# Three products of the recurrence's preparation issued on VectorE instead of GpSimd, and seven PSUM tiles instead of three for the block products of the first rotary pass

## The chip, the cores and the metric

The kernel runs on one core of a Trainium2 chip. The metric is the device time of one execution in microseconds (us); the time before is the median of three runs. The engines are named as the profile names them: PE is TensorE (PEld its weight loads), DVE is VectorE, ACT is ScalarE, POOL is GpSimd, SP issues the DMAs.

## The reference, cut to what matters

One layer over 2048 latent and 256 context tokens of width 1024: normalisation and modulation, an input projection to 3232 columns, of which 1696 go through a depthwise convolution into a bidirectional RWKV-7 mixer and 1536 into differential attention with rotary queries and keys; an output projection and a gated MLP follow. Two parts are touched.

```python
def apply_rope(x, cos, sin):
    half = DIFF_HEAD // 2
    x1, x2 = x[..., :half], x[..., half:]
    return jnp.concatenate([x1 * cos - x2 * sin, x1 * sin + x2 * cos], axis=-1).astype(x.dtype)
...
# rwkv_prepare, for each of the two directions
w = -jax.nn.softplus(-(w0 + w_lat @ w2).astype(jnp.float32)) - 0.5
decay = jnp.exp(-jnp.exp(w))
a = jax.nn.sigmoid((a0 + al @ a2).astype(jnp.float32))
k_dir = k * (1.0 + (a - 1.0) * p['k_a'])
```

The kernel runs the recurrence in chunks of 64 tokens. So per direction it needs the running products W of the decays within a chunk, their reciprocals IW, and these scaled operands: kk times a and k times (1+(a-1)k_a), both times IW (the tile G), and kk and r times W (the tile Q).

## The kernel before, in words

`phase1` (line 198) makes the normalised, transposed activations in two groups: blocks 0 to 2 (the 256 context tokens and two blocks of 512 latent tokens), later blocks 3 and 4. It projects 128 columns at a time: `wnext` hands out a weight tile split into two parts, `wH` (ACT, L232) and `wL` (POOL, L233), and `mtile` (L244) multiplies it with one block in 24 matmuls (L34 to L36) into a PSUM tile `mm`. The pool of `mm` tiles, `psmm`, has three.

For group 0 come first the columns of the attention's values, then eight column tiles through `rope_tile` (L383), 20 block products. ACT copies four swapped quarters out of `mm` into `rsw` (L401), DVE multiplies `mm` by the cosine (L405), `rsw` by the sine (L406) and adds (L407). `mm` is free after L401 and L405. In the same stretch `mod_chunk` (L124) makes eight pieces of the modulation: DVE accumulates 64 weight tiles `mww` into `macc` (L136), and a small product `mg` (L142, L149) on PE sums each piece over the partitions.

Then come the convolution columns: `tile_a` for blocks 0 to 2, `tile_b` for blocks 3 and 4 and the held-back block 2. ACT evacuates `mm` (L602). `piece` (L544) convolves: ACT one tap (L550), DVE two (L551, L552), into `cout`, or into `okt` for the four column tiles of keys. For a key piece ACT then makes `kk` (L564) and its square `ksq` (L566), PE sums the squares into `pn` (L570), DVE and POOL make the reciprocal norm `krn` (L572, L573), PE spreads it (L578), DVE multiplies (L579). `prep` (L495) follows, once for each direction:

- PE: two small products `pk` (L517); ACT: tanh (L519), sigmoid's shift (L521);
- DVE: the running sum `cs` (L523); ACT: W and IW (L524, L525), the last column of W (L527);
- DVE: first half of `G` (L529); ACT: (1+(a-1)k_a) into `ta` (L530); **POOL: second half of `G` (L531)**; DVE: `G` times IW (L532); SP: `G` to HBM (L533);
- **POOL: `Q` from `kk` (L535)**; ACT: one column of `Q` (L536); **POOL: `Q` from `rr` or `kk` (L537)**; SP: `Q` to HBM (L538).

There are 4 key column tiles and 5 blocks, so 40 directions: 32 with 512 tokens and 8 with the 256 of the context. `G`, `Q` and the inputs `t` have two buffers each.

The second rotary pass (blocks 3 and 4) runs through the same `rope_tile` at the end of `phase1`, while `phase2b` begins. The order in each engine's queue isn't written out: the framework's scheduler sets it when the program is built (L1898), engine by engine, from its own estimate of durations. Each engine then works its queue strictly in order.

Of the kernel before, what the change touches and what calls it, by code (L numbers as in the profile page):

```python
# [8 lines left out]
F32 = mybir.dt.float32  # L9
# [3 lines left out]
ALU = mybir.AluOpType  # L13
AX = mybir.AxisListType
PSUM = bass.MemoryType.PSUM
DRAM = bass.MemoryType.DRAM

P = 128
# [9 lines left out]
BLK = 512  # L28
CH = 64
# [3 lines left out]
def split_mm(nc, out, lH, lL, rH, rL, first, last):  # L33
    nc.tensor.matmul(out, lhsT=lH, rhs=rH, start=first, stop=False)  # L34
    nc.tensor.matmul(out, lhsT=lH, rhs=rL, start=False, stop=False)  # L35
    nc.tensor.matmul(out, lhsT=lL, rhs=rH, start=False, stop=last)  # L36
# [161 lines left out]
def phase1(tc, I, T, pr, ident, bones, keep):  # L198
    nc = tc.nc
    with ExitStack() as st:  # L200
        def rpool(stack, name, bufs, **k):
            return stack.enter_context(tc.tile_pool(name=name, bufs=bufs, side="right", **k))
# [3 lines left out]
        ps = rpool(st, "psmm", 3, space=PSUM)  # L206
# [11 lines left out]
        seq_b = [1536] + [c for j in range(4) for c in (j * P, (4 + j) * P, vcol + j * P, (8 + j) * P)] + [1600] + rope_cols  # L218
        order = v_cols + rope_cols + seq_a + seq_b
        raws, ready = [], []  # L220

        def wload():
            raw = mp.tile([P, KT, P], F32, name="wraw", bufs=1)
            c0 = order.pop(0)
            nc.sync.dma_start(out=raw, in_=wv[:, :, c0:c0 + P])
            raws.append(raw)
# [9 lines left out]
        def wnext():  # L236
            W = ready.pop(0)
            if raws:
                wsplit()
            if order:  # L240
                wload()
            return W

        def mtile(W, b):  # L244
            n = BLOCKS[b][1]
            o = ps.tile([P, BLK], F32, name="mm")
            mtile.out = o
            for k in range(KT):
                split_mm(nc, o[:, 0:n], W[0][:, k], W[1][:, k], hH[b][:, k], hL[b][:, k], k == 0, k == KT - 1)
                if k % 2 and k < KT - 1:  # L250
                    yield

        def mfull(W, b):
            for _ in mtile(W, b):
                pass
            return mtile.out

        def vblock(vp, pv, tags, W, j, b):
            t0, n = BLOCKS[b]
            yield from mtile(W, b)  # L260
            o = mtile.out
            S = vp(tags[0])
            nc.vector.tensor_copy(out=S[:, 0:n], in_=o[:, 0:n])
            yield
            tp = pv.tile([P, BLK], F32, name=tags[1])
            for t in range(n // P):
                nc.tensor.transpose(out=tp[:, t * P:(t + 1) * P], in_=S[:, t * P:(t + 1) * P], identity=ident)
            V = vp(tags[2])
            nc.vector.tensor_copy(out=V[:, 0:n], in_=tp[:, 0:n])
            nc.sync.dma_start(out=T["vd"][t0:t0 + n, j * P:(j + 1) * P].rearrange("(t p) c -> p t c", p=P),  # L270
                              in_=V[:, 0:n].rearrange("p (t c) -> p t c", c=P))
            yield
# [33 lines left out]
        with ExitStack() as s2:  # L306
# [68 lines left out]
            for j in (2, 3):  # L375
                W = wnext()
# [34 lines left out]
        def load_cs(pool, group):  # L411
            lat = [b for b in group if b]
            cs = pool.tile([P, 2, len(lat), BLK], F32, name="cossin")
            nc.sync.dma_start(out=cs, in_=I["rope"][:, :, BLOCKS[lat[0]][0] - CTX:BLOCKS[lat[-1]][0] + BLK - CTX].rearrange("a p (b t) -> p a b t", t=BLK))
            return cs

        with ExitStack() as s4:
            rp = rpool(s4, "ropep", 3)
            rc = rpool(s4, "ropec", 1)
            pv = rpool(s4, "psr", 1, space=PSUM)  # L420
            cs = load_cs(rc, GROUPS[0])
            ones = rc.tile([P, P], F32, name="mones")
            nc.gpsimd.memset(ones, 1.0)

            def mods():
                for part in (2, 3, 4, 5):
                    for hf in range(2):
                        yield from mod_chunk(nc, I, T, col, rp, rc, pv, "mg", sC[:, :, 0], keep, part, hf, ones)
            mg = mods()

            def mstep():
                for _ in range(6):
                    next(mg, None)

            for c0 in rope_cols:
                for _ in rope_tile(c0, GROUPS[0], cs, lambda n: rp.tile([P, BLK], F32, name=n), ("rst", "rsw"), mstep):
                    pass
            nc.sync.dma_start(**late.pop())
            for _ in range(1000):
                next(mg, None)  # L440

        with ExitStack() as s3:
            cp = rpool(s3, "convp", 2)
# [25 lines left out]
            for d, s in enumerate(("fwd", "bwd")):  # L469
# [7 lines left out]
                W = W4[:, d]  # L477
# [17 lines left out]
            def prep(h, b, O, K):  # L495
                t0, n = BLOCKS[b]
                m = n // CH
                rr = K
                if b:
                    rr = cp.tile([P, BLK], F32, name="rr", bufs=2)  # L500
                    nc.sync.dma_start(out=rr, in_=T["rwT"][h * P:(h + 1) * P, t0:t0 + n])
                for d in range(2):
                    i0 = t0 // CH
                    if d:
                        i0 = 0 if b == 0 else 36 + 4 - i0 - m

                    def v(ap):
                        ap = ap[:, 0:n]
                        return ap[:, ::-1] if d else ap

                    def c(ap):
                        return ap[:, 0:n].rearrange("p (m t) -> p m t", t=CH)

                    t = []
                    for e in range(2):
                        z = pv.tile([P, BLK], F32, name="pk")
                        nc.tensor.matmul(z[:, 0:n], lhsT=W4[:, d, e, h * P:(h + 1) * P], rhs=los[b][:, e], start=True, stop=True)  # L517
                        t.append(cp.tile([P, BLK], F32, name="t%d" % e, bufs=2))
                        nc.scalar.activation(out=t[e][:, 0:n], in_=v(z), func=AF.Tanh, scale=0.5)  # L519
                    sg, ta = t  # L520
                    nc.scalar.activation(out=sg[:, 0:n], in_=sg[:, 0:n], func=AF.Identity, scale=0.5, bias=half)  # L521
                    cs = cp.tile([P, BLK], F32, name="cs", bufs=2)
                    nc.vector.tensor_tensor_scan(out=cs[:, 0:n], data0=smask[:, 0:n], data1=sg[:, 0:n], initial=0.0, op0=ALU.mult, op1=ALU.add)  # L523
                    nc.scalar.activation(out=sg[:, 0:n], in_=cs[:, 0:n], func=AF.Exp, scale=-CDEC)  # L524
                    nc.scalar.activation(out=cs[:, 0:n], in_=cs[:, 0:n], func=AF.Exp, scale=CDEC)  # L525
                    W, IW = c(sg), c(cs)
                    nc.scalar.copy(out=pr.wc[:, i0:i0 + m, d, h], in_=W[:, :, CH - 1])  # L527
                    G = cp.tile([P, 2 * BLK], F32, name="G", bufs=2)[:, 0:2 * n].rearrange("p (m e t) -> p m e t", e=2, t=CH)
                    nc.vector.scalar_tensor_tensor(out=G[:, :, 0], in0=c(ta), scalar=1.0, in1=c(v(K)), op0=ALU.add, op1=ALU.mult)  # L529
                    nc.scalar.activation(out=ta[:, 0:n], in_=ta[:, 0:n], func=AF.Identity, scale=hka[:, h:h + 1], bias=oka[:, h:h + 1])  # L530
                    nc.gpsimd.tensor_tensor(out=G[:, :, 1], in0=c(v(O)), in1=c(ta), op=ALU.mult)  # L531
                    nc.vector.tensor_tensor(out=G, in0=G, in1=IW.unsqueeze(2).broadcast_to([P, m, 2, CH]), op=ALU.mult)  # L532
                    nc.sync.dma_start(out=T["pd"][d * 4 + h, :, i0 * P:(i0 + m) * P], in_=G.rearrange("p m e t -> p (m e t)"))  # L533
                    Q = cp.tile([P, 2 * BLK], F32, name="Q", bufs=2)[:, 0:2 * n].rearrange("p (m t) -> p m t", t=P)
                    nc.gpsimd.tensor_tensor(out=Q[:, :, 1:CH], in0=c(v(K))[:, :, 1:CH], in1=W[:, :, 0:CH - 1], op=ALU.mult)  # L535
                    nc.scalar.copy(out=Q[:, :, 0:1], in_=c(v(K))[:, :, 0:1])  # L536
                    nc.gpsimd.tensor_tensor(out=Q[:, :, CH:P], in0=c(v(rr)), in1=W, op=ALU.mult)  # L537
                    nc.sync.dma_start(out=T["qd"][d * 4 + h, :, i0 * P:(i0 + m) * P], in_=Q.rearrange("p m t -> p (m t)"))  # L538
                    yield

# [151 lines left out]
            for c0 in seq_b[1:]:  # L692
                if c0 >= vcol:
                    W = wnext()
# [18 lines left out]
G = 3  # L713
# [243 lines left out]
CH = 64  # L957
# [859 lines left out]
def build(tc, I, out):  # L1817
    nc = tc.nc
    with ExitStack() as st:
# [20 lines left out]
        for ev in phase1(tc, I, T, pr, ident, bones, keep):  # L1840
            if ev == "early":
                next(p2b)
                early = iter(lambda: next(p2b), "main")
            elif early:
                for _ in range(2):
                    next(early, None)
# [55 lines left out]
```

## Time and profile before

| | |
|---|---|
| median of three runs | 4119.32 us (4115.85 to 4120.19) |
| the profiled execution's own time | 4121.25 us |
| its span, first to last instruction | 4119.5 us |
| PE busy | 3798.8 us, 92% |
| DVE, ACT, POOL busy | 63%, 47%, 37% |
| mean granted TensorE clock | 0.955 |

The stages that the change touches, in us from the span's start: first rotary pass 133 to 264; `tile_a` 264 to 470; the transposes of group 1 470 to 540; `tile_b` 540 to 822; second rotary pass 822 to 930. The rows further down give start, busy time of each engine and idle time; in a row of the timeline or of the groups, "idle before" is the time for which the engine stood still just before, and behind "<-" stands what ended it.

### The profile page before, as it was taken

To read this page: it belongs to the slowest core of one execution; us is meant where nothing else is said; L and a number is where in the kernel's file an instruction comes from. 1 tells how busy PE (TensorE), PEld (TensorE's weight loads), DVE (VectorE), ACT (ScalarE), POOL (GpSimd) and SP (SyncE) were. 2 spreads that over 40 slices of the span, in tenths; PEclk is the share of its full clock that TensorE was granted. 3 is DMA by queue.
4 is the path that set the end of the run, shared out by engine and by line. 5 is a ranking of instruction groups with operands and counts; after the bars stand their busy time and mean duration, and the time that the engine had idled before them with its cause. 6 is when DMAs were issued, how large, how long until landed. Compare 5 with 4: busy or idle time off the path is not lost. (4 is left out here: it accounts for less than half of the span.)

```text
span 4119.5 us, 65492 instructions
## 1 busy us (share of the span) xinstructions
PE 3798.8 (92%) x25471; PEld 3218.9 (78%) x25471; DVE 2601.3 (63%) x3781; ACT 1925.6 (47%) x3806; POOL 1511.7 (37%) x1578
## 2 busy tenths in 40 slices
PE   7999888887999886899999889999999999999999
PEld 4777677676888776889898867778888888878887
DVE  3466566778889985888889877754444444420243
ACT  4236556666666655677777744622112112221211
POOL 3236466734444433454544356510111111022222
PEclk8999899998999988999999989999999999999999
DMA  5554546644433433020102164411111111131333
GB/s 175 156 172 163 164 157 220 212 136 96 99 93 97 97 80 97 14 61 9 48 6 63 47 202 137 151 57 45 53 46 54 51 47 47 51 105 50 111 120 104
DMA packets 464724, 400.80 MB, mean 97 GB/s; under 512 B 131613, under 2 KB 393702, under 8 KB 463390
## 3 DMA queue, kind: packets, MB, share of 16 engines
q1 hardware_dynamic: 464414, 396.61, 31.5%
q8 instruction: 201, 3.29, 0.4%
q14 instruction: 109, 0.89, 0.1%
HBM read 269.51 MB, written 131.74 MB: 97 GB/s over the span
## 5 line engine op out<-in xcount | busy, mean ns | idle before, releaser
L34 PE MATMUL o<-h2H,wuH 128*128 128x512 f32 x1920 | 750.9, 392 | 5.7 <-DVE h2H L179 4.0
L35 PE MATMUL o<-h2L,wuH 128*128 128x512 f32 x1920 | 751.4, 391 | 0.4 <-DVE h2L L180 0.2
L36 PE MATMUL o<-h2H,wuL 128*128 128x512 f32 x1920 | 750.4, 391 | 1.2 <-POOL wuL L1607 1.2
L1607 POOL TENSOR_TENSOR wuL<-wuraw,wuH 128x1024 fp32r<-128x1024 f32 x76 | 183.6, 2417 | 840.4 <-ACT wuH L1606 840.4
L34 PEld LDWEIGHTS o<-h2H,wuH 128*128 128x128 f32 x1920 | 361.0, 188 | 84.0 <-DVE h2H L179 4.2
L36 PEld LDWEIGHTS o<-h2H,wuL 128*128 128x128 f32 x1920 | 361.2, 188 | 78.7 <-POOL wuL L1607 1.7
L35 PEld LDWEIGHTS o<-h2L,wuH 128*128 128x128 f32 x1920 | 361.3, 188 | 78.4 <-DVE h2L L180 1.0
L34 PE MATMUL mm<-hH,wH 128*128 128x512 f32 (+1 forms) x968 | 381.4, 395 | 15.6 <-DVE rst L405 9.8
L802 DVE TENSOR_REDUCE nb<-S 128x1 f32<-128x768 f32 x384 | 357.9, 948 | 58.5 <-PE S L801 57.3
L803 ACT ACTIVATE P<-S,nb 128x768 f32<-128x768 f32 x384 | 345.8, 907 | 77.0 <-DVE nb L802 73.9
L35 PE MATMUL mm<-hL,wH 128*128 128x512 f32 (+1 forms) x968 | 378.1, 391 | 0.1
L36 PE MATMUL mm<-hH,wL 128*128 128x512 f32 (+1 forms) x968 | 376.3, 389 | 0.5 <-POOL wL L233 0.5
L800 PE MATMUL S<-kH,qs 128*128 128x384 f32 x768 | 293.5, 382 | 34.9 <-ACT P L803 34.4
L844 PE MATMUL pv<-V,aT 128*128 128x128 f32 x2304 | 309.4, 278 | 6.4 <-DVE O L860 3.3
L1627 ACT COPY cs<-o 128x512 f32<-128x512 f32 x176 | 102.9, 585 | 450.6 <-PE o L36 448.1
L844 PEld LDWEIGHTS pv<-V,aT 128*128 128x128 f32 x2304 | 285.8, 194 | 10.2 <-DVE O L860 6.3
L801 PE MATMUL S<-kL,qs 128*128 128x384 f32 x768 | 261.3, 340 | 0.0
L830 DVE SCALAR_TENSOR_TENSOR P<-P,f,P 128x768 f32<-128x768 f32 x192 | 244.1, 1284 | 12.9 <-POOL P L828 11.6
L34 PEld LDWEIGHTS mm<-hH,wH 128*128 128x128 f32 x968 | 190.7, 198 | 53.4 <-DVE rst L405 10.6
L36 PEld LDWEIGHTS mm<-hH,wL 128*128 128x128 f32 x968 | 190.2, 196 | 37.5 <-issue 1.0
L35 PEld LDWEIGHTS mm<-hL,wH 128*128 128x128 f32 x968 | 191.0, 197 | 35.2 <-issue 0.7
L852 ACT COPY aT<-tpa 128x512 f32<-128x512 f32 (+1 forms) x320 | 173.6, 542 | 93.7 <-PE tpa L851 90.9
(372 smaller groups left out, 8039.2 us busy)
## 6 DMA issues: line engine op xcount, KB each, us to landing
wraw<-in_w_in_dram SPq DMA_DIRECT2D x52, 512.0 KB
wuraw<-in_w_up_dram SPq DMA_DIRECT2D x44, 512.0 KB
scr_actT<-wuH SPq DMA_DIRECT2D x44, 512.0 KB
QP<-scr_qd SPq DMA_DIRECT2D x36, 512.0 KB
PK<-scr_pd SPq DMA_DIRECT2D x144, 128.0 KB
mww<-in_w_mod_dram SPq DMA_DIRECT2D x64, 256.0 KB
scr_qd<-Q SPq DMA_DIRECT2D x32, 512.0 KB
scr_pd<-G SPq DMA_DIRECT2D x32, 512.0 KB
```

The costliest lines, as they stand in the source:

```text
L34: nc.tensor.matmul(out, lhsT=lH, rhs=rH, start=first, stop=False)
L35: nc.tensor.matmul(out, lhsT=lH, rhs=rL, start=False, stop=False)
L36: nc.tensor.matmul(out, lhsT=lL, rhs=rH, start=False, stop=last)
L800: nc.tensor.matmul(S[:, b, 0:HB], lhsT=qs[:, qt * P:(qt + 1) * P], rhs=kH[:, sl], start=True, stop=False)
L801: nc.tensor.matmul(S[:, b, 0:HB], lhsT=qs[:, qt * P:(qt + 1) * P], rhs=kL[:, sl], start=False, stop=True)
L802: nc.vector.tensor_reduce(out=nb[:, m, g:g + 1], in_=S[:, :, 0:HB], op=ALU.max, axis=AX.XY, negate=True)
L803: nc.scalar.activation(out=Pm[m][:, g * GW:(g + 1) * GW].rearrange("p (b x) -> p b x", b=2), in_=S[:, :, 0:HB], func=AF.Exp, bias=nb[:, m, ...
L830: nc.vector.scalar_tensor_tensor(out=Pm[0][:, sls[g - 1]], in0=Pm[0][:, sls[g - 1]], scalar=f[:, 0, g - 1:g], in1=Pm[1][:, sls[g - 1]], op ...
L844: nc.tensor.matmul(pv, lhsT=aT[:, j], rhs=V[:, k0 + j], start=(k0 + j == 0), stop=(k0 + j == KTT - 1))
L852: nc.scalar.copy(out=aT[:, 0:n], in_=tp[:, 0:n])
L1607: eng.tensor_tensor(out=L, in0=raw, in1=H.bitcast(F32), op=ALU.subtract)
L1627: nc.scalar.copy(out=S[:, 1 + b * BLK:1 + (b + 1) * BLK], in_=o)
```

## The change

Three `tensor_tensor` products of `prep` (L531, L535, L537) are issued on DVE instead of POOL, 120 instructions in all. For the first rotary pass alone, `mtile` takes its PSUM tiles in turn from two pools, the three of `psmm` and four of a new pool `psx`; afterwards the list is set back to three.

```diff
         raws, ready = [], []
+        ring = [ps] * 3
...
             n = BLOCKS[b][1]
-            o = ps.tile([P, BLK], F32, name="mm")
+            ring.append(ring.pop(0))
+            o = ring[-1].tile([P, BLK], F32, name="mm")
...
             pv = rpool(s4, "psr", 1, space=PSUM)
+            ring.extend([rpool(s4, "psx", 4, space=PSUM)] * 4)
...
             for _ in range(1000):
                 next(mg, None)
+            ring[:] = [ps] * 3
...
-                    nc.gpsimd.tensor_tensor(out=G[:, :, 1], in0=c(v(O)), in1=c(ta), op=ALU.mult)
+                    nc.vector.tensor_tensor(out=G[:, :, 1], in0=c(v(O)), in1=c(ta), op=ALU.mult)
...
-                    nc.gpsimd.tensor_tensor(out=Q[:, :, 1:CH], in0=c(v(K))[:, :, 1:CH], in1=W[:, :, 0:CH - 1], op=ALU.mult)
+                    nc.vector.tensor_tensor(out=Q[:, :, 1:CH], in0=c(v(K))[:, :, 1:CH], in1=W[:, :, 0:CH - 1], op=ALU.mult)
...
-                    nc.gpsimd.tensor_tensor(out=Q[:, :, CH:P], in0=c(v(rr)), in1=W, op=ALU.mult)
+                    nc.vector.tensor_tensor(out=Q[:, :, CH:P], in0=c(v(rr)), in1=W, op=ALU.mult)
```

The scheduler is run anew, so the queues of all engines are ordered anew. Lines of the changed kernel lie 1 to 4 higher (L531 is L535, L552 is L556). Two places show what moved.

PE, the first rotary pass, the start of the block product that begins at 249.9 us in the trace: `hH_294` is the context block, `hH_360` block 1; a matmul's own wait stands behind it. Before:

```order
L35 MATMUL mm<-hL_295,wH 128x256
L36 MATMUL mm<-hH_294,wL 128x256
L34 MATMUL mm<-hH_360,wH 128x512 [waits DVE_49]
L35 MATMUL mm<-hL_361,wH 128x512
L36 MATMUL mm<-hH_360,wL 128x512
```

The same place of the changed kernel:

```order
L35 MATMUL mm<-hL_295,wH 128x256
L36 MATMUL mm<-hH_294,wL 128x256
L34 MATMUL mm<-hH_360,wH 128x512
L35 MATMUL mm<-hL_361,wH 128x512
L36 MATMUL mm<-hH_360,wL 128x512
```

The order is the same; the wait for DVE is gone. Of the other block products of this pass that waited for DVE alone, one still does (the first into a tile of the new pool); the waits for ACT and POOL at a new weight tile stay.

DVE, `tile_b`, the last rows up to the `okt` row (second tap) of the fourth key tile, for which the next `pn` waits. Before:

```order
L613 COPY kk<-pk 128x512
L523 SCALAR_TENSOR_TENSOR cs<-smask,t_5842 128x512
L529 SCALAR_TENSOR_TENSOR G<-t_5846,kk 128x8x64
L551 SCALAR_TENSOR_TENSOR cout<-cst,cols,cout 128x512
L532 TENSOR_TENSOR G<-G,cs 128x1024
L552 SCALAR_TENSOR_TENSOR cout<-cst,cols,cout 128x512
L551 SCALAR_TENSOR_TENSOR cout<-cst,cols,cout 128x512
L552 SCALAR_TENSOR_TENSOR cout<-cst,cols,cout 128x512
L551 SCALAR_TENSOR_TENSOR cout<-cst,cols,cout 128x512
L552 SCALAR_TENSOR_TENSOR okt<-cst,cols,okt 128x512
```

The same place of the changed kernel:

```order
L555 SCALAR_TENSOR_TENSOR cout<-cst,cols,cout 128x512
L533 SCALAR_TENSOR_TENSOR G<-t_5306,kk 128x8x64
L535 TENSOR_TENSOR G<-okt,t_5281 128x8x64
L556 SCALAR_TENSOR_TENSOR cout<-cst,cols,cout 128x512
L555 SCALAR_TENSOR_TENSOR cout<-cst,cols,cout 128x512
L536 TENSOR_TENSOR G<-G,cs 128x1024
L539 TENSOR_TENSOR Q<-kk,t_5302 128x8x63
L541 TENSOR_TENSOR Q<-rr,t_5302 128x8x64
L555 SCALAR_TENSOR_TENSOR cout<-cst,cols,cout 128x512
L556 SCALAR_TENSOR_TENSOR cout<-cst,cols,cout 128x512
L535 TENSOR_TENSOR G<-okt,t_5306 128x8x64
L556 SCALAR_TENSOR_TENSOR okt<-cst,cols,okt 128x512
```

Four of the moved products stand among the last twelve rows ahead of that `okt` row. From the third `krn` row of the second key tile to the `okt` row of the third, 17 of the tile's 18 moved products stand in DVE's queue. On PE the first `pn` of the second, third and fourth key tile of `tile_b` stands behind 2008, 2200 and 2392 of the 2904 block matmuls before, and behind 2012, 2213 and 2410 now.

## Rows read from the trace of the kernel before

**Rows 1.** The core's span and mean granted clock.

```profile
core 0: 4119.5 us, clock 0.955
```

**Rows 2.** Busy time in stretches; columns: stretch, length, engines (instructions), clock, DMA.

```profile
125.00:300.00 175.00, 158.32 (x730) 130.75 (x729) 103.46 (x132) 59.38 (x94) 41.76 (x28) 0.93 0.57 171
...
349.80:382.00 32.20, 31.32 (x146) 26.29 (x145) 21.65 (x22) 20.74 (x48) 21.97 (x19) 0.89 0.51 174
...
688.60:757.00 68.40, 58.03 (x263) 46.85 (x264) 50.24 (x44) 42.74 (x81) 47.52 (x28) 0.92 0.63 214
```

**Rows 3.** What PE waited for, 125 to 300 us: total, times, longest.

```profile
PE mm L34 <- DVE rst L405: 7.1, 2, 5.5
PE mg L149 <- issue: 5.3, 2, 2.8
PE mg L142 <- issue: 2.9, 1, 2.9
```

**Rows 4.** Timeline of PE in `tile_b`: start, duration, instruction, idle before.

```profile
618.89 1.87 PE L570 MATMUL pn<-bones,ksq 128*128 128x2 f32 x8 [6.09 <-ACT ksq L566]
```

**Rows 5.** Stretches around the two kinds of stop (columns as in Rows 2).

```profile
244.40:249.90 5.50, 0.04 (x1) 0.00 (x0) 3.36 (x3) 3.73 (x6) 2.34 (x1) 0.78 0.53 181
249.90:252.10 2.20, 2.19 (x5) 1.82 (x6) 2.20 (x4) 0.00 (x0) 0.00 (x0) 0.50 0.41 119
252.10:259.00 6.90, 6.90 (x31) 5.71 (x31) 3.83 (x7) 1.21 (x3) 0.47 (x1) 0.84 0.72 193
...
618.80:620.80 2.00, 1.91 (x9) 1.91 (x10) 1.08 (x2) 0.04 (x1) 0.00 (x0) 0.50 1.01 300
620.80:631.00 10.20, 10.20 (x40) 8.29 (x41) 4.14 (x5) 4.95 (x7) 5.71 (x4) 0.73 0.99 349
```

**Rows 6.** Groups of DVE, 125 to 270 us: count, busy, mean ns, idle before.

```profile
L136 DVE SCALAR_TENSOR_TENSOR macc<-mww,sC,macc 128x512 f32<-128x512 f32 x60 | 55.7, 931 | 32.4 <-DMA mww<-in_w_mod_dram 31.5 <-issue 0.3 <-DMA macc<-in_b_mod_dram 0.3
```

**Rows 7.** Timelines of DVE and POOL, some rows where both are busy.

```profile
608.98 1.76 DVE L551 SCALAR_TENSOR_TENSOR cout<-cst,cols,cout 128x512 f32<-128x512 f32 x1
610.66 2.31 DVE L532 TENSOR_TENSOR G<-G,cs 128x1024 f32<-128x1024 f32 x1
...
608.47 1.72 POOL L535 TENSOR_TENSOR Q<-kk,t 128x504 f32<-128x504 f32 x1
610.15 1.73 POOL L537 TENSOR_TENSOR Q<-rr,t 128x512 f32<-128x512 f32 x1
```

**Rows 8.** The same timelines, rows where only one of the two works.

```profile
661.39 1.21 DVE L523 TENSOR_TENSOR_SCAN cs<-smask,t 128x512 f32<-128x512 f32 x1
662.52 0.66 DVE L529 SCALAR_TENSOR_TENSOR G<-t,kk 128x512 f32<-128x512 f32 x1
683.05 0.74 DVE L551 SCALAR_TENSOR_TENSOR cout<-cst,cols,cout 128x512 f32<-128x512 f32 x1
686.48 1.22 DVE L532 TENSOR_TENSOR G<-G,cs 128x1024 f32<-128x1024 f32 x1
...
663.40 1.26 POOL L535 TENSOR_TENSOR Q<-kk,t 128x504 f32<-128x504 f32 x1 [1.72 <-ACT t L524]
```

**Rows 9.** Line 407, a two-input product on DVE: shortest, median, longest ns.

```profile
L407 DVE TENSOR_TENSOR rst<-rst,rsw x32: 651/684/1669, 152.1 to 932.4; 128x512 f32<-128x512 f32 x32
```

**Rows 10.** From the third `krn` to the next `okt`: stretch (columns as in Rows 2).

```profile
637.72:685.90 48.18, 39.02 (x178) 30.45 (x176) 38.44 (x33) 30.20 (x61) 40.61 (x23) 0.98 0.53 183
```

**Rows 11.** The same stretch: a group of POOL, and what DVE waited for.

```profile
L233 POOL TENSOR_TENSOR wL<-wraw,wH 128x1024 fp32r<-128x1024 f32 x3 | 9.4, 3141 | 6.4 <-ACT wH L232 6.3
...
DVE G L529 <- DMA scr_pd<-G: 5.2, 3, 2.6
```

**Rows 12.** Timeline of POOL, a weight split beside little DVE work.

```profile
622.32 2.38 POOL L233 TENSOR_TENSOR wL<-wraw,wH 128x1024 fp32r<-128x1024 f32 x1 [4.02 <-ACT wH L232]
```

## Prediction

> **What bounds the kernel now.** I took the span and the clock first [rows 1], then busy time by stage [rows 2], then PE's waits where the change acts. PE is the busiest engine everywhere, so a microsecond counts only if PE stands still for it or runs slowly after it.
>
> In the first rotary pass PE waits 7.1 us in two places for DVE's cosine product, which frees an `mm` tile, and 8.2 us for the modulation's `mg` products [rows 3]. The longer of the two, 5.5 us, ends at 249.9; the granted clock is 0.50 (1.2 GHz) just after it and 0.84 over the next 6.9 us [rows 5]. That costs 2.2 x 0.50 + 6.9 x 0.16 = 2.2 us more.
>
> In `tile_b` each key column tile takes some 68.4 us, with PE busy 58.0 of them at clock 0.92 [rows 2]. The largest loss is one stop of 6.1 us at `pn` for ACT's `ksq` [rows 4], which came late because DVE's `okt` row did; two of the other three key tiles show the same stop. Behind it the clock is 0.50 for 2.0 us and 0.73 for 10.2 us [rows 5], another 1.0 + 2.75 = 3.75 us. So such a stop costs 9.9 us.
>
> Why is `okt` late? From the third `krn` to the next `okt` row 48.2 us pass, in which DVE is busy 38.4 and POOL 40.6 [rows 10]. Both run long. Where they meet, their instructions take turns: a tap takes 1.76 us and a product on POOL 1.72 to 1.73 [rows 7], against 0.74 and 1.26 where the other engine is quiet [rows 8]. So POOL's products are not free cover. They lengthen DVE's queue.
>
> **The seven tiles.** The order shows that the block product at 249.9 loses its wait for DVE. Its weights were in use already, so nothing else holds it: 5.5 + 2.2 = 7.7 us. The shorter wait, 7.1 - 5.5 = 1.6 us, lies ahead of `mg` products that PE waits for anyway [rows 3], so I count nothing for it. The last `mg` products come earlier on PE too, but their accumulations are paced by loads: DVE stands idle 32.4 us before them in this stretch, 31.5 of it for `mww` [rows 6]. I give 1.7 us back to them and take **6 us**. Bounds: 7.1 + 2.2 = 9.3 us, and nothing if the modulation takes all.
>
> **The three products, tile_b.** Removed from POOL per key tile: 18 products of at least 1.26 us, 22.7 us. Added to DVE: 18 of 0.68, the median of a two-input product of the same size [rows 9], 12.2 us. The moved ones read reversed or strided operands in part; L529 does so already at 0.66 [rows 8].
>
> What matters is the stretch up to `okt`. DVE's 33 instructions there [rows 10] are, by its order, 5 running sums of 1.21, 5 products over 1024 of 1.22, 5 first halves of 0.66, 13 taps of 0.74 [rows 8], 4 single copies or PSUM products of about 0.68 and one small row: 27.9 us unhindered. They were busy 38.4, so POOL cost DVE 10.5 us, and DVE stood idle 48.2 - 38.4 = 9.7. Now 17 of the 18 products stand ahead of `okt` in the order: 27.9 + 17 x 0.68 = 39.5 us. What is left on POOL there is three weight splits of 2.38 [rows 12] (3.14 when hindered [rows 11]), at most 7.1 us of blocking. The idle time is waits for ACT and 5.2 us for `G`'s store to leave its buffer [rows 11]; before, POOL worked meanwhile, now DVE's own products can fill it.
>
> - Floor: no blocking and no idle time, 39.5 us.
> - Ceiling: all of both, 39.5 + 7.1 + 9.7 = 56.3 us.
> - Taken: half of each, 39.5 + 3.6 + 4.9 = 48.0 us, because the queue is denser but strictly in order and `ta`, W and IW still come from ACT.
>
> That is 48.2 before and 48.0 after. The moved products replace on DVE what POOL had cost it. The gain comes mainly from `pn`, which stands 4, 13 and 18 block matmuls later in the order by the second, third and fourth tile: 18/3 x 0.23 us = 1.4 us a tile of useful matmuls ahead of the wait. The stop shrinks by 0.2 + 1.4 = 1.6 us, and I count 0.9 for the shorter slow stretch. **2.5 us for each of four key tiles: 10 us.**
>
> The Trainium skill's page SBUF — State Buffer, section on SBUF's two separate sides, states that a DVE instruction with two SBUF inputs and a GpSimd instruction lock each other out for the whole instruction. Had every blocking to be paid and no idle time, that rule would make the stretch 46.6 us; rows 7 agree with it.
>
> **The three products, tile_a.** Per key tile a context block and a full block: 6 products on half the tokens and 6 on all. DVE is busy 21.7 of 32.2 us and POOL 22.0, PE 31.3 at clock 0.89 [rows 2]. The loss that could come back is 0.9 + 0.11 x 32.2 = 4.4 us a tile. DVE has room here, but the order moves some `pn` a few matmuls forward as well. I take 0.75 us each, **3 us** for four; bounds 18 us and nothing.
>
> **At nothing:** the time in which POOL now stands idle, since what is left on it waits for ACT (6.4 us before the weight splits [rows 11]) and PE not for it; if that cover goes, a split is late by no more than its own 2.38 us; the reordering after 930 us, where the queues hold the same instructions in nearly the same order (I allow 4 us either way).
>
> **Sum.** 6 + 10 + 3 = 19 us off the profiled execution's 4121.3 gives 4102; the median of the three runs lies 1.9 us under that execution, so **4100 us**. This case alone reaches from 4088 to 4110.
>
> **Rivals.**
>
> *The locked port was the bound.* Then the floor holds: 39.5 us in `tile_b`, the stop disappears and the clock stays up. Gain: four times 9.9 us, half of tile_a's 18, and 9.3 in the rotary pass: 39.6 + 9 + 9.3 = 58, so 4061 us. For it: one or the other of DVE and POOL is busy nearly all of that stretch, 38.4 + 40.6 in 48.2 us [rows 10]. Against: DVE's waits for ACT and for stores don't go away.
>
> *DVE's single queue becomes the bound, slower than before.* Each moved product waits in order for ACT's `ta` or W, and the taps of the next key tile are queued behind it. If the full 9.7 us of idle time stays beside the products and every weight split blocks, the stretch is 56.3 us: 8.1 longer, less the 1.4 by which `pn` moved, 6.7 for each of four tiles, 27 us; less 6 of the rotary pass, 4119 + 21 = 4140 us. It decides from 39.5 + 7.1 + w = 48.2 + 1.4 + 9/4, that is from w = 5.2 of the 9.7 us. Before, DVE's wait of 5.2 us for stores alone [rows 11] is of that size.
>
> *The products move, and nothing follows.* DVE's stretch stays and so does the stop; only the rotary pass gives: 4113 us, and less if the modulation takes it. The Trainium skill's page Perfetto Trace Analysis, section Optimizing Scalar/DVE Operations, speaks for this one: GpSimd and DVE share a read port, so shifting operations between those two might not help.
>
> **How the numbers follow.** Chances: forecast 0.50, port 0.17, queue 0.17, nothing follows 0.16. A measurement of this kernel tells a change from none at about 0.2%, 8 us. Faster by over that, below 4111: the forecast and the port, 0.67. Within: 0.16. Slower, above 4127: 0.17. The range for 8 in 10 takes in the forecast, the case of nothing, most of the port's case and the mild half of the queue's: 4062 to 4130 us. Faster holds most of the chance, and the likeliest case's own range is 4088 to 4110.
>
> **What would show it.** Right: no wait of a block matmul for L405 (now L407) in the first rotary pass and no 0.50 clock near 250 us; the moved products at about 0.68 us on DVE; taps and running sums back near 0.74 and 1.21 except beside weight splits; DVE's busy time in `tile_a` and `tile_b` about as before, POOL's lower by 180 us; the stops at `pn` some 4 us instead of 6. Wrong: stops at `pn` of 8 us or more with DVE busy throughout (queue), no stops at all (port), or waits at `mg` that grow by what the ring saves.

## The result, and the profile after

The changed kernel takes **4060.63 us** (median of 4 runs, 4056.87 to 4067.3), against 4117.59 for the kernel before on the same chip (4 runs, 4114.12 to 4120.19): ratio **0.9864**, 95% interval 0.9847 to 0.9881. It is 57 us faster. The forecast was 19 us, so the sign was right and the size was wrong, by more than the range allowed.

The core's span and clock [rows 1]:

```profile
core 0: 4065.5 us, clock 0.959
```

Where did the time go? I followed marks that exist in every kernel: the start of the n-th matmul of the block products on PE (counted from 0), the first S of the attention, and the end. The 768th block matmul is the first behind the first rotary pass, the 1039th comes just after the first `prep` of `tile_a` has begun, the 1608th ends `tile_a`, the 2570th ends `tile_b`, the 2903rd ends the second rotary pass; then comes the chunk recurrence. Each kernel of interest was profiled once, these two a second time (us of each stretch):

| stretch | before | again | after | again | products alone | tiles alone |
|---|---|---|---|---|---|---|
| up to the first `prep` | 328.4 | 326.2 | 328.2 | 325.3 | 328.0 | 324.7 |
| `tile_a` from there | 139.7 | 139.4 | 129.8 | 131.3 | 133.1 | 139.9 |
| to the end of `tile_b` | 350.8 | 350.4 | 316.1 | 317.0 | 313.8 | 351.2 |
| second rotary pass | 107.1 | 109.8 | 109.0 | 111.7 | 114.0 | 106.4 |
| chunk recurrence | 658.5 | 652.5 | 644.1 | 637.4 | 634.5 | 644.8 |
| attention to the end | 2535.0 | 2532.1 | 2538.3 | 2536.4 | 2530.0 | 2528.8 |

By the two pairs: nothing up to the first `prep`, -8 to -10 us in `tile_a`, -33 to -35 in `tile_b`, and -14 to -15 in the recurrence, which the change doesn't touch; the second rotary pass is 2 us longer and the attention 3 to 4. Part of `tile_b`'s figure comes from where the mark lies: before, 24 small products of the recurrence (`pa`, 2.7 us of PE) stand ahead of the 2570th block matmul, after the change they stand behind it. From the 1608th to the 2600th, with the same number of PE instructions on both sides, the gain is 32 to 33 us.

The stages in windows (columns as in [rows 2]), the kernel before first, `tile_b`'s four key tiles and then `tile_a`:

```profile
552.10:818.90 266.80, 231.01 (x1046) 186.11 (x1047) 195.61 (x170) 168.06 (x319) 189.31 (x110) 0.92 0.59 200
328.40:468.10 139.70, 134.50 (x674) 113.63 (x673) 92.12 (x89) 81.95 (x184) 85.58 (x73) 0.95 0.55 179
```

The changed kernel, the same block products:

```profile
539.40:774.00 234.60, 219.61 (x1023) 179.37 (x1023) 196.15 (x240) 167.89 (x319) 70.04 (x38) 0.96 0.68 230
328.20:457.90 129.70, 127.51 (x674) 108.72 (x673) 92.04 (x135) 84.14 (x187) 32.66 (x30) 1.00 0.61 197
```

DVE has 70 and 46 more instructions and not a microsecond more of busy time; POOL lost 172 us. In `tile_b` PE's idle time fell from 266.8 - 231.0 = 35.8 to 15.0 us, and its busy time by 11.4 us: 20.8 + 11.4 = 32.2 us. Of the 11.4, 2.7 us are the recurrence's 24 products, which lie in the window before and not in the one after; the other 8.7 go with the clock, which rose from 0.92 to 0.96. In `tile_a` PE's shorter busy time, at a clock of 1.00 instead of 0.95, gave 7.0 of 10.0 us.

What PE waited for in `tile_b`, before (552.1 to 818.9):

```profile
PE pn L570 <- ACT ksq L566: 18.0, 3, 6.1
PE pk L611 <- ACT t L519: 5.6, 4, 3.5
```

and after (539.4 to 774):

```profile
PE pk L582 <- ACT ksq L578: 4.8, 5, 1.7
PE mm L34 <- ACT ksq L611: 3.8, 1, 3.8
PE mm L34 <- ACT cst L606: 3.4, 2, 2.2
PE pn L574 <- DVE krn L576: 2.9, 1, 2.9
```

The three stops at `pn` for `ksq` [rows 4] are gone altogether, not shortened. Why, the stretch from the third `krn` to the next `okt` [rows 10] tells:

```profile
618.54:656.80 38.26, 36.91 (x167) 30.40 (x168) 38.09 (x50) 28.72 (x59) 8.04 (x4) 0.96 0.76 259
```

It is 38.3 us instead of 48.2, with DVE busy for 38.1 of them. Some of DVE's rows in it:

```profile
623.29 0.68 DVE L535 TENSOR_TENSOR G<-okt,t 128x512 f32<-128x512 f32 x1
623.89 0.74 DVE L556 SCALAR_TENSOR_TENSOR cout<-cst,cols,cout 128x512 f32<-128x512 f32 x1
624.55 1.21 DVE L536 TENSOR_TENSOR G<-G,cs 128x1024 f32<-128x1024 f32 x1
...
628.32 2.81 DVE L533 SCALAR_TENSOR_TENSOR G<-t,kk 128x512 f32<-128x512 f32 x1
...
646.53 2.83 DVE L555 SCALAR_TENSOR_TENSOR cout<-cst,cols,cout 128x512 f32<-128x512 f32 x1
```

and POOL's two large ones:

```profile
628.17 2.40 POOL L234 TENSOR_TENSOR wL<-wraw,wH 128x1024 fp32r<-128x1024 f32 x1 [7.45 <-PE pk L521]
...
645.28 3.53 POOL L234 TENSOR_TENSOR wL<-wraw,wH 128x1024 fp32r<-128x1024 f32 x1 [8.96 <-DMA scr_pd<-G]
```

The turn-taking of [rows 7] is left only where a weight split runs: two DVE instructions of 2.81 and 2.83 us. All others are at the unhindered durations of [rows 8], the moved products at 0.65 to 0.68.

In the first rotary pass (125 to 300 us) the waits for DVE's cosine product [rows 3] are gone, and those for `mg` have more than taken their place, 17.5 us on these two rows against 8.2 before:

```profile
PE mg L142 <- issue: 10.4, 2, 7.6
PE mg L149 <- issue: 7.1, 2, 4.6
```

The pass's own block products did end earlier: the 768th block matmul starts at 257.6 us instead of 264.3. The 6.7 us are lost at the last `mg`, which stands behind the 831st in PE's queue. DVE's last accumulation, which that product reads, comes no earlier, before and after:

```profile
276.11 0.75 DVE L136 SCALAR_TENSOR_TENSOR macc<-mww,sC,macc 128x512 f32<-128x512 f32 x1 [1.60 <-DMA mww<-in_w_mod_dram]
```

```profile
276.77 0.75 DVE L136 SCALAR_TENSOR_TENSOR macc<-mww,sC,macc 128x512 f32<-128x512 f32 x1 [2.73 <-DMA mww<-in_w_mod_dram]
```

In the changed kernel it ends at 277.5, and `mg` begins at 277.6, after the wait of 7.6 us, which the profile puts down to "issue". The 846th block matmul, behind that product, starts at 285.7 us instead of 282.7.

### The profile page after: what moved, and what is told of

It reads as the page before. It is cut to its first block, busy times and chain, and to the rows that moved or that the text cites. A ratio compares the mean times of both kernels' runs of the same rounds, so it can differ in the third digit from the quotient of the medians.

```text
span 4065.5 us, 65448 instructions
## 1 busy us (share of the span) xinstructions
PE 3783.3 (93%) x25471; PEld 3211.0 (79%) x25471; DVE 2596.7 (64%) x3901; ACT 1924.6 (47%) x3806; POOL 1331.2 (33%) x1458
## 5 line engine op out<-in xcount | busy, mean ns | idle before, releaser
L234 POOL TENSOR_TENSOR wL<-wraw,wH 128x1024 fp32r<-128x1024 f32 x52 | 139.6, 2684 | 291.6 <-ACT wH L233 263.0
```

Source lines behind the costliest of these rows:

```text
L234: nc.gpsimd.tensor_tensor(out=L, in0=raw, in1=H.bitcast(F32), op=ALU.subtract)
```

## The experiments

Theory **L**: a POOL product with two operands and a DVE instruction of this kind exclude each other, so POOL's 120 products were lengthening DVE's queue, and that queue the stops of PE. Theory **M**: in the first rotary pass the modulation's loads are the pace, so the seven tiles find nothing to give. Theory **R**: the recurrence is shorter because the scheduler laid its instructions in another order. The rivals stand with each run.

### The two parts apart

Products alone, on a ring of three (the other two products in the same way):

```diff
-nc.gpsimd.tensor_tensor(out=G[:, :, 1], in0=c(v(O)), in1=c(ta), op=ALU.mult)
+nc.vector.tensor_tensor(out=G[:, :, 1], in0=c(v(O)), in1=c(ta), op=ALU.mult)
```

> The three products on VectorE, the first rotary pass with three PSUM tiles as before. Theory L (the two engines no longer lock each other out, and this alone gave the gain): the block products of tile_a and tile_b end 40 to 46 us earlier as in the changed kernel, time 4055 to 4068. Theory T (the seven tiles have a share of 6 to 9 us): 4067 to 4072. In both the waits for mg in the first rotary pass are back to some 8 us and the wait for L405 to 7 us.

Measured: 4059.56 us (4054.96 to 4065.38; before in that job 4115.55), ratio 0.9864 [0.9845, 0.9884]. The products alone give a gain as large as the whole change.

Seven tiles alone:

```diff
+ring.extend([rpool(s4, "psx", 4, space=PSUM)] * 4)
```

> The seven PSUM tiles alone, the products on GpSimd. Theory M (the modulation's loads pace the first rotary pass, so PE waits at mg for what it no longer waits for at the tiles): the last block product of that pass ends within 3 us of before, waits at mg 16 to 21 us, time 4111 to 4123. Theory T (the tiles give 6 to 9 us): 4108 to 4112.

Measured: 4101.28 us, ratio 0.9962 [0.9946, 0.9978]. Below what any theory expected. By the table the stretch up to the first `prep` and the two tile stages give little (2 to 4 us, and nothing); 8 to 14 us lie in the recurrence (644.8 us). So the time was no sign of the ring's own worth, and a third theory was needed (below).

### Is it POOL's products, or the order?

The changed kernel, with POOL made to repeat the three products on three quarters of the columns, into a tile that nobody reads:

```diff
+dz = cp.tile([P, 6, CH], BF16, name="dz", bufs=1)[:, 0:min(m, 6)]
+nc.gpsimd.tensor_tensor(out=dz, in0=c(v(O))[:, 0:min(m, 6)], in1=c(ta)[:, 0:min(m, 6)], op=ALU.mult)
```

(and likewise behind Q's two products).

> The changed kernel, and GpSimd computes the three products a second time, on three quarters of the columns, into a tile that nobody reads. VectorE's own list of work is that of the changed kernel. Theory L (lock): VectorE's products, taps and sums are stretched again, by more than before since VectorE has more work; stops at pn come back; tile_a and tile_b take as long as before or longer, time 4110 to 4150. Theory O (the gain came from the new order of the queues, not from the lock): 4058 to 4075.

Measured: 4140.05 us, ratio 1.0061 [1.0042, 1.008]: 80 us slower than the change, slower even than before. `tile_b` and `tile_a`:

```profile
571.50:855.20 283.70, 235.11 (x1023) 187.94 (x1024) 245.10 (x237) 168.88 (x318) 166.30 (x108) 0.90 0.56 187
328.30:485.90 157.60, 140.72 (x675) 117.48 (x673) 122.94 (x136) 85.52 (x187) 83.50 (x74) 0.91 0.55 160
```

DVE does the same work as in the changed kernel and is busy 245.1 us for 196.2 in `tile_b`, 122.9 for 92.0 in `tile_a`. And the stops are back:

```profile
PE pn L578 <- ACT ksq L574: 21.3, 3, 7.2
PE pk L521 <- DVE kk L587: 12.3, 5, 4.5
```

Over one key tile's stretch (597 to 656.7 us in the changed kernel, 707 to 778.6 here) the same six products on DVE take, in the changed kernel and then here:

```profile
L535 DVE TENSOR_TENSOR G<-okt,t 128x512 f32<-128x512 f32 x6 | 4.0, 674 | 0.0
```

```profile
L535 DVE TENSOR_TENSOR G<-okt,t 128x512 f32<-128x512 f32 x6 | 7.1, 1191 | 0.0
```

What POOL computes there is read by nobody. The small `krn` product and the weight splits queue behind it on POOL and come later, and the queues are ordered anew; that could delay PE, but it doesn't explain why a row of DVE's, once begun, lasts longer. Theory L holds. A third of the dose the other way, only G's second half moved (its one line as above, ring of three):

> One of the three products per direction alone (the second half of G, 40 of 120) goes to DVE, over the ring of three; Q's two stay on POOL. Moving all three over the ring of three brought the end of tile_a and tile_b forward by 43.9 us. Theory L (while POOL has a two-operand product under way, DVE's two-operand work stands, and the reverse, so each product moved gives back its share): about a third, 10 to 18 us, by the end of tile_b, and 4090 to 4106 us in all. Rival S (only the stop at pn for ksq counts, and it goes when G's chain ahead of the next okt row is short enough; G's half is the one that G's own second product waits for): most of the gain, 30 us or more by the end of tile_b, below 4090 us. Rival N (a threshold is not reached): under 5 us.

Measured: 4096.15 us, ratio 0.9943 [0.9928, 0.9958]. The end of `tile_b` comes 20.9 us earlier, 15.3 of it behind the first `prep`, where all three gave 43.6: a third of the products, 35% of the gain (or 40%, 15.5 of 38.7 us, up to the 2600th block matmul, with the same number of PE instructions in all three kernels). The stops at `pn` in `tile_b` shrink instead of going:

```profile
PE pn L570 <- ACT ksq L566: 12.1, 3, 4.2
```

The total lies in L's band; the early 20.9 us lie a little above it, by the 5.6 us ahead of that start, for which I have no explanation beyond the 2 to 3 us by which one kernel differs from itself there. Rivals S (all or nothing) and N fall.

### What paces the first rotary pass

The changed kernel with six buffers for the modulation's loads and three accumulators:

```diff
-acc = cp.tile([P, BLK], F32, name="macc", bufs=2)
+acc = cp.tile([P, BLK], F32, name="macc", bufs=3)
-w = wp.tile([P, BLK], F32, name="mww")
+w = wp.tile([P, BLK], F32, name="mww", bufs=6)
```

> The changed kernel with six buffers instead of three for the modulation's weight tiles, and three instead of two accumulators. Theory M: the accumulations run ahead of PE, the waits at mg fall from 20 us to below 8, the first rotary pass ends 8 to 20 us earlier, time 4040 to 4054. Rival (the loads are bound by the DMA engines' bandwidth, not by buffers): no change, 4056 to 4066.

Measured: 4050.25 us, ratio 0.9844 [0.9821, 0.9866]. The 846th block matmul, three block products behind the pass, starts at 261.7 us instead of 285.7, 24 us earlier and more than expected; 9 to 16 us are lost again in the recurrence (653.1 us). DVE's accumulations in the changed kernel, 125 us to that matmul, and then in this one:

```profile
L136 DVE SCALAR_TENSOR_TENSOR macc<-mww,sC,macc 128x512 f32<-128x512 f32 x64 | 53.2, 834 | 40.3 <-DMA mww<-in_w_mod_dram 34.2 <-DMA macc<-in_b_mod_dram 3.3 <-POOL macc L127 2.3
```

```profile
L136 DVE SCALAR_TENSOR_TENSOR macc<-mww,sC,macc 128x512 f32<-128x512 f32 x64 | 51.9, 826 | 13.4 <-DMA mww<-in_w_mod_dram 7.5 <-issue 4.5 <-DMA macc<-in_b_mod_dram 0.7
```

Idle time for `mww` falls from 34.2 to 7.5 us, and PE's wait for `mg` from 17.5 to 4.2 us on the rows shown above. To see whether the seven tiles are worth anything once the loads are out of the way, the same buffers in the kernel before, and with the seven tiles:

> The kernel before with six instead of three buffers for the modulation's loads and three instead of two accumulators; ring of three, products on POOL. Theory M (in the first rotary pass PE is paced by the modulation's loads, the ring of three only by what is left): the 846th block matmul, at 282.7 us in the kernel before, starts 10 to 18 us earlier, the waits for the modulation's products fall under 3 us, and waits for DVE's rst product of 6 us or more stay. Rival D (DVE's rotary products are the pace at three tiles, so that loads coming earlier only move the wait to them): under 6 us earlier, waits for rst of 15 us or more. The total follows with whatever order the chunk recurrence gets, which in the four kernels so far was worth 5 to 24 us.

> The same buffers for the modulation, and the seven tiles; products on POOL. Theory M: with the loads out of the way the seven tiles give what was forecast of them, the 846th block matmul starts 5 to 10 us before that of the same kernel with a ring of three. Rival (the seven tiles give nothing whatever the loads do): within 2 us of it.

Measured: 4091.14 us (ratio 0.993 [0.9915, 0.9945]) and 4089.59 us (0.993 [0.991, 0.9949]). PE's waits in the pass with three tiles:

```profile
PE mm L34 <- DVE rst L405: 9.0, 4, 4.0
```

and with seven:

```profile
PE mg L142 <- issue: 4.8, 1, 4.8
```

The 846th block matmul starts at 268.8 and 264.8 us. So M holds (14 us from the loads), and the seven tiles are worth 4 us after all where the loads are out of the way, between the two expectations. At the end nothing of it can be told. Last, buffers and products without the seven tiles:

> More buffers for the modulation (six and three), the three products on DVE, and the ring of three. The same with seven tiles took 4050.25 us. The two runs with products on POOL showed the seven tiles ending the first rotary pass 4 us earlier, and nothing of it left at the end of the kernel. Theory M: the first pass ends 3 to 6 us after that of the same kernel with seven tiles, the total is 4046 to 4056 us. Rival (with DVE emptier or fuller the ring matters more): 8 us or more later in the pass, and 4058 us or more in all.

Measured: 4054.61 us, ratio 0.9844 [0.9827, 0.9861], the same ratio as with them; the 846th block matmul starts at 269.4 us. That is 7.7 us later than with seven tiles, near the rival's 8, but the total is in M's band. With the modulation's buffers the medians lie 6 to 10 us below the changed kernel's, with the seven tiles and without. But the intervals of the ratios overlap (0.9821 to 0.9866 and 0.9827 to 0.9861, against 0.9847 to 0.9881): that these two beat it is likely, not shown.

### The recurrence

The changed kernel, with the modulation's products asked for one step earlier:

```diff
-    for _ in range(4):
+    for _ in range(3):
```

> The changed kernel with the modulation's products asked for one step earlier (three instead of four). That is nearly nothing in the first 930 us, but in it the chunk recurrence, which the change doesn't touch, comes out in the row order of the kernel before (5074 of 5086 PE rows match; 4230 for the changed kernel). From the end of the second rotary pass to the first S of the attention it took 658.5 us in the kernel before, 644.1 in the changed one, 634.5 with the products alone, 644.8 with the seven tiles alone and 653.1 with more buffers, which has the order of the kernel before too. Theory R (the order in which the scheduler lays the recurrence's instructions costs those microseconds): 651 to 660 us. Rival K (it is shorter because of what comes ahead of it): 642 to 647 us. Total by R 4066 to 4076, by K 4058 to 4064 us.

Measured: 4076.38 us, ratio 0.9894 [0.9879, 0.9909]; the recurrence took 648.9 us. That lies between the two expectations. The total lies at R's end, but 5.6 us of it are not the recurrence's: the second rotary pass ended that much later than in the changed kernel, so the edit was not nothing ahead of it. So I measured how far one kernel differs from itself, and tried another order behind an unchanged first part (one priority in phase2b):

```diff
-OFF = dict(C=0, A=1000, I=0, G=4500, E=5500)
+OFF = dict(C=0, A=900, I=0, G=4500, E=5500)
```

> The kernel before, unchanged, in a second profiled execution on another day of the same study. The chunk recurrence, from the end of the second rotary pass to the attention's first S, took 658.5 us in the first one (4121.3 us, 3.7 above the median). Three kernels whose recurrence has this row order or nearly so took 658.5, 653.1 and 648.8. Theory E (executions of one kernel differ there by several microseconds, and the profile of before was a long one): 648 to 655 us, and an execution of 4112 to 4119 us. Theory R (the row order sets it): 656 us or more.

> The changed kernel, unchanged, in a second profiled execution. Recurrence 644.1 us in the first. Theory E: anywhere from 640 to 650, at a distance of less than 6 us from the repeat of the kernel before. Theory R: 642 to 646, and 10 us or more below the repeat of the kernel before. Up to the end of tile_b (818.9 us in the kernel before, 774.0 in the changed one) both theories expect the same within 3 us.

> The kernel before with one priority of the chunk recurrence changed (assembly 900 instead of 1000): every PE row ahead of the recurrence stands where it stood, the recurrence itself is laid out in another order (2211 of its 5086 PE rows match in sequence). Theory R: the recurrence takes 5 us or more, less or more, than in the repeat of the kernel before, and the total moves with it. Theory E: within 4 us of it, and the total within 0.1 per cent of the kernel before.

Measured: 652.5, 637.4 and 648.6 us; 4112.22 and 4060.92 us for the two repeats, and for the new order 4116.8 us, ratio 0.9996 [0.9985, 1.0006]. One kernel differs from itself by 6 to 7 us here, as E says. But the distance between before and after is 14.4 us in the first pair and 15.1 in the second, as R says. The last run went as E says: 3.9 us from the repeat, and the same total. So not every other order gives something.

PE's idle time in the recurrence separates the two. The kernel before and its repeat, then the changed kernel and its repeat, then the one with the earlier `mg` (columns as in [rows 2]):

```profile
926.00:1584.50 658.50, 559.42 (x9059) 498.96 (x9057) 550.37 (x1339) 410.58 (x930) 277.88 (x341) 0.88 0.38 93
925.80:1578.30 652.50, 554.85 (x9059) 494.54 (x9057) 550.87 (x1339) 410.32 (x930) 277.27 (x341) 0.89 0.38 93
```

```profile
883.10:1527.20 644.10, 559.52 (x9059) 500.29 (x9057) 544.20 (x1338) 409.21 (x928) 276.59 (x341) 0.88 0.39 94
885.20:1522.60 637.40, 553.01 (x9059) 493.51 (x9057) 543.71 (x1338) 409.00 (x928) 276.93 (x341) 0.89 0.39 95
```

```profile
888.70:1537.60 648.90, 552.30 (x9058) 492.85 (x9057) 550.09 (x1337) 410.81 (x930) 277.51 (x341) 0.90 0.39 94
```

Length less busy time is 99.1 and 97.6 us before, 84.6 and 84.4 after. The busy times of the two kernels agree within 2 us in each pair. So 13 to 15 us of the distance are waits of PE, and most of the 6 to 7 us between two executions of one kernel is busy time. With the earlier `mg`, where the recurrence has the order of the kernel before behind the products of the changed one, PE is idle for 96.6 us: the waits go with the order, as R says. In the last run they come to 100.9 us, so its order saves none; its recurrence is short by its busy time, 547.7 us.

What differs can be seen in the last 30 us of the recurrence. In the kernel before (1555 to 1585 us):

```profile
1570.43 0.68 PE L1148 MATMUL pc<-Zk,Tb 64*64 64x64 f32 x16
1576.87 1.12 PE L1148 MATMUL pc<-Zk,Tb 64*64 64x64 f32 x16 [5.75 <-DVE Zk L1135]
...
1583.05 1.51 PE L1168 MATMUL py<-AP,X 64*64 64x64 f32 x16 [4.21 <-ACT X L1150]
```

In the changed kernel:

```profile
1519.73 1.15 PE L1152 MATMUL pc<-Zk,Tb 64*64 64x64 f32 x32
1524.91 2.32 PE L1172 MATMUL py<-AP,X 64*64 64x64 f32 x32 [4.03 <-ACT X L1154]
```

In the kernel with the modulation's buffers:

```profile
1500.31 0.68 PE L1152 MATMUL pc<-Zk,Tb 64*64 64x64 f32 x16
1506.45 1.12 PE L1152 MATMUL pc<-Zk,Tb 64*64 64x64 f32 x16 [5.46 <-DVE Zk L1139]
```

Before, the two directions' last products stand apart, and the second waits 5.5 to 5.8 us; after, they stand together, x32, and don't wait. Over the last 70 us PE is idle 23.7 to 24.8 us in the four profiles with that wait (before twice, the modulation's buffers, the early `mg`) and 15.3 and 17.9 in the two of the change, 13.3 and 12.0 with the products or the tiles alone. So 6 to 9 us of the 14 are the order at the tail; that the kernel with the earlier `mg` got the long form from an edit elsewhere shows that the order is a by-product. In which of the recurrence's waits the rest of the 14 lies stays open.

## Why the prediction was wrong

**What bounds the kernel** was read rightly: the stop at `pn` for `ksq` behind a late `okt`, with POOL's products in DVE's way. It went when they did, and came back when POOL was given such products again.

**The three products, tile_b: "Taken: half of each, 39.5 + 3.6 + 4.9 = 48.0 us".** This step failed. The stretch took 38.3 us, below the floor. The idle time that I left at 4.9 us of 9.7 was 0.2: the moved products and what they no longer hold up fill DVE's queue, and no instruction in it waited for ACT or a store for long. The blocking, taken as 3.6, was (2.81 - 0.67) + (2.83 - 0.74) = 4.2 us. And 39.5 us was too high a floor: the rows of DVE's instructions overlap where they follow without a gap (0.68 us long, the next begins 0.60 us after it); in this stretch the overlaps add up to 3.5 us, and four running sums began in it, not five. I had the mechanism, turn-taking, and halved its effect out of caution: the rows behind [rows 10] show one or the other of the two engines busy for 47.9 of the 48.2 us, which means that work taken off one is time. The gain was 29.5 us for the four tiles (the 32.2 above without the recurrence's 2.7) instead of 10. The rival *the locked port was the bound* named the right outcome, "no stops at all", at 9.9 us for each tile; it was 7.4.

The Trainium skill's page SBUF — State Buffer, section on SBUF's two separate sides, has the exclusive lock; the traces agree: DVE's 0.67 us instruction lasts 2.81 beside a split of 2.40 that began 0.15 us before it. The Trainium skill's page Perfetto Trace Analysis, section Optimizing Scalar/DVE Operations, says that moving work between GpSimd and DVE might not help; here it helped by 1.36%, since a product takes 1.26 us on POOL [rows 8] and 0.68 on DVE, and the two add up either way.

**tile_a, 3 us taken, bounds 18 and nothing:** 8 to 10 us. The term was mis-sized: 7.0 us of it is the clock, back from 0.95 to 1.00, of which I counted little; PE's idle time gave the other 3.0.

**The seven tiles, "6 us".** The pass's own block products ended 6.7 us earlier, with no wait for L407 and a clock of 1.00 from 240 to 262 us, but nothing of it was left behind the last `mg`. The step that failed is "I give 1.7 us back to them": the `mg` waits took back everything, 8.2 us before and 17.5 after. [Rows 6] held the answer: where DVE is idle 31.5 us for `mww`, PE gains nothing from reaching `mg` sooner. The prediction's own last sign of being wrong, "waits at `mg` that grow by what the ring saves", is what the trace shows.

**After 930 us, "±4".** Wrong: 14 to 15 us in the recurrence, nearly all of it waits of PE. "The same instructions in nearly the same order" was a reading of the counts; in sequence 4230 of 5086 PE instructions of the recurrence matched.

**The sum.** The port rival gave 4061 us and 4060.63 was measured, but its terms were not those: 48.6 us in the tile stages (measured 40 to 43, up to the 2600th block matmul), 9.3 in the rotary pass (nothing left behind its last `mg`), nothing in the recurrence (14 to 15). The errors cancelled. Of the signs: DVE's busy time stayed as forecast (287.7 and 288.2 us over both tile stages), POOL's fell by 172 of the forecast 180. The rivals *queue* and *nothing follows* fell.

## What to carry to other kernels

Where DVE and POOL take turns in the rows and one or the other is busy all the time, count them as one engine: the price of a POOL product is then its whole duration, and moving it to DVE gains the difference at once, idle time included. Reckoned so after the fact, the 17 products in the stretch up to `okt` are worth 17 x (1.26 - 0.68) = 9.9 us, an estimate from [rows 8] and [rows 9]; the stretch went from 48.2 to 38.3 us. Before widening a buffer for one wait, look at what the pass waits for next; if that is a load, widen the load's buffers first. A scheduler that works from modelled times can lay a far stage anew for any edit, so split a measured gain by stages before crediting it to the edit.

## What the runs showed of the hardware

- Where one DVE instruction follows another without a gap, rows of 0.68 us begin 0.60 us apart (623.29 and 623.89 above), so sums of durations come out too long, by 3.5 of 41.6 us in the stretch shown.
- The lock works both ways: a weight split that takes 2.40 us on POOL took 3.53 us at 645.28, in the same stretch in which it held DVE's tap for 2.83 us.
- Two executions of one kernel differed by 6.0 and 6.7 us in the recurrence, and in the tile stages by 1.5 us at most.
